# Queries and keys of a hybrid attention block projected with features on partitions, the scale of a query taken into the exponential

## The chip, the cores and the metric

The kernel runs as one program on one core of a Trainium2 chip. A core has five engines that work side by side, each through its own instructions in order: TensorE (PE in the profile; PEld is its weight load), VectorE (DVE), ScalarE (ACT), GpSimd (POOL) and SyncE (SP, which here issues transfers). They meet in the on-chip memories SBUF (128 partitions) and PSUM (128 partitions, banks of 512 float32) and wait for each other by semaphores. The metric is the device time of one execution in microseconds (us), as the median of several runs.

## The reference

A decoder block for 512 tokens of width 1024, in float32. What matters here is the sparse attention branch, one of two that run on the same normalised input:

```python
q = _rms_norm(q.reshape(B, S, ATTN_HEADS, ATTN_HEAD_DIM), attn_q_norm[l])
k = _rms_norm(k.reshape(B, S, ATTN_HEADS, ATTN_HEAD_DIM), attn_k_norm[l])
...
scores = jnp.einsum('bqhs,bqh->bqs', head_scores, wib) * IDX_HEADS ** -0.5
_, sel = lax.top_k(scores, topk)
...
logits = jnp.einsum('bqhd,bqkhd->bhqk', qb, k_sel).astype(f32) * scale
logits = logits + jnp.transpose(bias, (0, 3, 1, 2))
probs = jax.nn.softmax(logits, axis=-1).astype(v.dtype)
```

There are 8 heads of 64 features. Each head's query and key of a token is divided by the root mean square of its 64 features and multiplied by a gain per feature. An indexer scores the keys of each query, and each query attends to its 128 best keys.

## The kernel before

Every matrix product is made from three float32r products: activations and weights are split into a rounded part (`_hi`, `xnh`) and a remainder (`_lo`, `xnl`). The normalised input stands in SBUF with features on partitions. Weights stream in as chunks of 128x1024: SP issues the transfer into `w_raw`, ACT writes the rounded part `w_hi` (L241), and POOL (from the 18th chunk on every third one DVE) subtracts to get `w_lo` (L245). `w_hi` and `w_lo` have three buffers each.

Two helpers make products. `dense_t` keeps weights as the stationary operand, streams 512 tokens in one instruction and leaves features by tokens. `dense_k` keeps 128 tokens as the stationary operand, streams 256 columns of weights and leaves tokens by features. Queries, keys and values go through `dense_k` in that order, two calls of 256 columns each, from four chunks each.

For queries and keys each 128x256 piece of a result goes through `head_rms`. ACT copies it out of PSUM into `qraw` and squares it, DVE sums each head's 64 squares (L449), adds epsilon (L450), POOL raises to the power -0.5 (L452), and DVE multiplies the piece by that scale, one for each token and head (L453). Later, in `rest`, PE turns the piece over (`flip`, a transpose through the identity, L169), ACT writes the rounded part with the gain, and DVE the remainder (L465); keys get two more ACT copies (L467, L468). So the two flips of a piece wait for the chain ACT, DVE, POOL, DVE.

On the same DVE, at the same time, the indexer's choice runs. `scores` adds eight heads for each of three blocks of queries (256, 384 and 512 keys; L416 and L420, from `relu` tiles of ACT). `select` then makes 16 rounds for each block, each a search for the eight largest (L432) and their replacement (L433), and ends with a mask (L435). A block of `attention` needs its mask (`keep`); the first block needs none. Attention takes 32 units (four blocks by eight heads): PE makes logits, DVE adds a bias table `toep` and takes the maximum (L523 in the first block, L526 and L527 after it, L533 the sign), ACT takes the exponential (L534), PE flips it, and PE multiplies by values.

PE's order is written by hand: `Streams.run` hands PE to the part with the lowest rank that is due, by a clock of estimated PE times and by named signals; the delay `rms` in `L` says how long after its piece a `rest` may come. The order on the other engines is made by a scheduler with a timeline of its own. Each engine then executes strictly in that order.

## Time and profile before

| What | Value |
| --- | --- |
| Median of 3 runs | 963.98 us (963.55 to 964.72) |
| Profiled execution | 964.03 us, span of its trace 962.2 us |
| PE busy in the span | 915.0 us (95%) |
| DVE busy in the span | 435.9 us (45%) |
| ACT, POOL busy in the span | 350.6 us (36%), 372.3 us (39%) |

Shares over the whole span hide the stages: an engine that is busy for 45% of all can be the one that everything waits for during a tenth of it. The 40 slices of the page and busy times by window show this. "Idle before" is what an engine waited for just before an instruction. A waiting instruction holds up all behind it on its engine. A duration in the trace can hold a wait for a port that no semaphore shows, so durations of one kind are compared with each other.

### The profile page before, as it was taken

How to read it: one execution, taken by the hardware profiler on the slowest of the kernel's cores; microseconds unless marked ns; L12 is line 12 of the kernel's file. 1: busy time of each engine (PE TensorE's matmuls, PEld its weight loads, DVE VectorE, ACT ScalarE, POOL GpSimd, SP SyncE). 2: the span in 40 equal slices, each digit the busy share in tenths (PEclk: the TensorE clock that was granted, in tenths of full speed). 3: DMA queues.
4: the chain of work that ended last, by engine and by line, in shares of the span. 5: the costliest groups of instructions: out<-in, count | busy, mean ns of one | idle time of the engine just before them, and what ended most of it. 6: DMA issues, size and time to landing. Idle time of an engine off the chain costs nothing.

```text
span 962.2 us, 13991 instructions
## 1 busy us (share of the span) xinstructions
PE 915.0 (95%) x5670; PEld 779.0 (81%) x5670; DVE 435.9 (45%) x847; ACT 350.6 (36%) x596; POOL 372.3 (39%) x253
## 2 busy tenths in 40 slices
PE   6998777999999999999997999999999999999998
PEld 4997776888777778787886899888888888888886
DVE  5289999677466635765533715211111111101111
ACT  5454466544453433333323424332232323212120
POOL 6445441101357334444413733344444444432321
PEclk9998888999998999999998999999999999999999
DMA  6321232211212121011042222332223323223331
GB/s 230 80 89 44 67 88 66 66 45 44 77 45 66 44 81 53 24 45 44 23 143 77 88 88 69 95 100 88 99 98 92 106 88 110 88 95 102 132 110 44
DMA packets 24033, 77.80 MB, mean 81 GB/s; under 512 B 2726, under 2 KB 4223, under 8 KB 23969
## 3 DMA queue, kind: packets, MB, share of 16 engines
q1 hardware_dynamic: 20832, 72.56, 23.4%
q10 hardware_dynamic: 3136, 4.36, 1.6%
q8 instruction: 44, 0.72, 0.3%
q14 instruction: 21, 0.16, 0.1%
HBM read 74.53 MB, written 2.38 MB: 80 GB/s over the span
## 4 chain that ended last, share of the span: by engine, by line
PE 84%; DVE 11%; issue 2%; ACT 1%; POOL 1%; DMA 0%; ACTq 0%; DVEq 0%; POOLq 0%
PE ps_d L162 60%; PE ps_c L162 11%; PE ps_i L162 10%; DVE score L433 2%; PE ps_c L169 2%; DVE max L432 2%; DVE qraw L453 1%; DVE score L420 1%; DVE qs L465 1%; PE ps_i L169 1%; DVE qss L449 1%; DVE lg L527 1%; POOL w_lo L245 0%; DVE kl L465 0%; DVE xs L330 0%
## 5 line engine op out<-in xcount | busy, mean ns | idle before, releaser
L245 POOL TENSOR_TENSOR w_lo<-w_raw,w_hi 128x1024 fp32r<-128x1024 f32 (+1 forms) x94 | 222.0, 2364 | 387.5 <-ACT w_hi L241 383.9
L241 ACT ACTIVATE w_hi<-w_raw 128x1024 fp32r<-128x1024 f32 x129 | 136.6, 1059 | 346.5 <-PE ps_d L162 219.4
L162 PE MATMUL ps_d<-hnl,w_hi 128*128 128x512 f32 (+1 forms) x368 | 139.9, 380 | 0.4 <-DVE hnl L338 0.4
L162 PE MATMUL ps_d<-hnh,w_hi 128*128 128x512 f32 (+1 forms) x368 | 139.9, 380 | 0.0
L162 PE MATMUL ps_d<-hnh,w_lo 128*128 128x512 f32 (+1 forms) x368 | 139.8, 380 | 0.0
L162 PE MATMUL ps_d<-xnh,w_hi 128*128 128x512 f32 (+2 forms) x296 | 124.5, 420 | 0.0
L162 PE MATMUL ps_d<-xnh,w_lo 128*128 128x512 f32 (+2 forms) x296 | 112.8, 381 | 0.0
L162 PE MATMUL ps_d<-xnl,w_hi 128*128 128x512 f32 (+2 forms) x296 | 112.4, 380 | 0.0
L245 DVE TENSOR_TENSOR w_lo<-w_raw,w_hi 128x1024 fp32r<-128x1024 f32 x37 | 47.6, 1286 | 126.8 <-ACT w_hi L241 126.2
L1045 DVE TENSOR_TENSOR gsig<-ps_d,gsig 128x512 f32<-128x512 f32 x22 | 15.2, 692 | 157.6 <-PE ps_d L162 156.9
L162 PEld LDWEIGHTS ps_d<-hnl,w_hi 128*128 128x128 f32 x368 | 69.2, 188 | 13.4 <-DVE hnl L338 0.6
L162 PEld LDWEIGHTS ps_d<-hnh,w_lo 128*128 128x128 f32 x368 | 69.2, 188 | 13.2
L162 PEld LDWEIGHTS ps_d<-hnh,w_hi 128*128 128x128 f32 x368 | 69.2, 188 | 13.2
L162 PEld LDWEIGHTS ps_d<-xnh,w_hi 128*128 128x128 f32 x296 | 57.2, 193 | 10.0 <-issue 2.6
L162 PEld LDWEIGHTS ps_d<-xnh,w_lo 128*128 128x128 f32 x296 | 56.8, 192 | 10.5
L162 PEld LDWEIGHTS ps_d<-xnl,w_hi 128*128 128x128 f32 x296 | 57.2, 193 | 8.1 <-issue 1.9
L162 PE MATMUL ps_d<-w_hi,xnh 128*128 128x256 f32 x192 | 58.9, 307 | 0.0
L162 PE MATMUL ps_d<-w_lo,xnh 128*128 128x256 f32 x192 | 57.7, 301 | 0.0
L162 PE MATMUL ps_d<-w_hi,xnl 128*128 128x256 f32 x192 | 57.6, 300 | 0.0
L1049 POOL TENSOR_TENSOR ul<-gsig,uh 128x512 fp32r<-128x512 f32 x22 | 31.6, 1434 | 25.3 <-ACT uh L1048 25.3
L162 PEld LDWEIGHTS ps_d<-w_hi,xnh 128*128 128x128 f32 x192 | 40.8, 212 | 0.4
L162 PEld LDWEIGHTS ps_d<-w_lo,xnh 128*128 128x128 f32 x192 | 40.5, 211 | 0.4
(283 smaller groups left out, 1814.9 us busy)
## 6 DMA issues: line engine op xcount, KB each, us to landing
w_raw<-in_stream_dram SPq DMA_DIRECT2D x129, 512.0 KB, 3.5
xa<-in_x_dram SPq DMA_DIRECT2D x4, 512.0 KB, 6.5
ht<-in_x_dram ACTq DMA_DIRECT2D x8, 256.0 KB, 3.2
out_dram<-ht SPq DMA_DIRECT2D x8, 256.0 KB, 2.0
toep<-bias_table ACTq DMA_DIRECT2D x8, 128.0 KB, 2.6
gain<-in_rows_dram ACTq DMA_DIRECT2D x2, 256.0 KB, 4.2
con<-in_consts_dram SPq DMA_DIRECT2D x1, 321.0 KB
bias_table<-tab ACTq DMA_DIRECT2D x1, 276.0 KB
```

The lines of the kernel that those rows point to most:

```text
L162: nc.tensor.matmul(o, w, r, **kw)
L169: nc.tensor.transpose(o, src, idn)
L241: nc.scalar.activation(hi, raw, AF.Copy)
L245: eng.tensor_sub(lo[:, o:o + n_], raw[:, o:o + n_], hi[:, o:o + n_])
L420: nc.vector.scalar_tensor_tensor(sc, r, w, sc, op0=OP.mult, op1=OP.add)
L432: nc.vector.max(m8, sc)
L433: nc.vector.match_replace(sc, m8, sc, TAKEN)
L449: nc.vector.tensor_reduce(ss, hv(sq), axis=AX.X, op=OP.add)
L453: nc.vector.tensor_mul(hv(raw), hv(raw), rs[:, :, None].to_broadcast([128, 4, 64]))
L465: nc.vector.scalar_tensor_tensor(at_(lo, b), p2[a], gain[a], at_(hi, a), op0=OP.mult, op1=OP.subtract)
L1045: nc.vector.tensor_mul(g, pu, g)
L1049: nc.gpsimd.tensor_sub(ul, g, uh)
```

## The change

Queries and keys go through `dense_t`, a pair of chunks at a time, so that they come out of PE as features by tokens. Nothing of a query is flipped. A query isn't scaled: PE sums the squares of each head by a product with a 128x2 matrix of ones (`head_sums`, four instructions), DVE adds epsilon, and after the fourth piece POOL makes two 128x32 tables, the power -0.5 (the scale) and 0.5 (its inverse). The scale goes into the exponential as its `scale` operand and into the negated maximum, and the bias table is multiplied by the inverse before it is added. The first block's fused add and maximum becomes two instructions. A key's sums go through POOL as 128x8, ACT spreads them over 512 columns, PE flips that tile (four flips), and DVE multiplies the raw key by it, straight from PSUM. The remainder of a key is then the difference of two SBUF tiles. Attention waits for all queries and keys at once, where it waited block by block.

```diff
@@ -86,7 +86,7 @@
-L = dict(norm=3.0, normed=1.3, score=0.4, pick=0.15, rms=14.5, attn=0.6, attn_n=0.15, attn_out=2.0, sig=0.3,
+L = dict(norm=3.0, normed=1.3, score=0.4, pick=0.15, rms=6.5, sums=2.5, attn=0.6, attn_n=0.15, attn_out=2.0, sig=0.3,
          prep=5.0, knorm=6.5, bonus=6.0, mat=0.5, mats=2.8, inv_u=3.25, inv_t=1.4, inv_r=1.4, inv_n=0.9, inv_e=1.8,
...
@@ -225,8 +225,10 @@
...
-    mhalf = cp.tile([128, 8], F32, name="mhalf")
-    nc.gpsimd.memset(mhalf, -0.5)
+    half = cp.tile([128, 64], F32, name="half")
+    mhalf = half[:, 0:8]
+    nc.gpsimd.memset(half[:, 0:32], -0.5)
+    nc.gpsimd.memset(half[:, 32:64], 0.5)
@@ -438,39 +440,74 @@
     qs_, kh_, kl_ = big("qs", F32R), big("kh", F32R), big("kl", F32R)
-    pairs = lambda a: a.rearrange("q (p e) t -> q p e t", e=2)
     vt = [bp.tile([128, S], F32, name="vt", tag=tag, bufs=n) for tag, n in (("uu", 1), ("tt", 1), ("rr", 2), ("rr", 2))]
-    def head_rms(g, gain, name, t, ps):
-        raw, sq = [q for q in unit("qraw").rearrange("q (a b) -> a q b", a=2)]
-        nc.scalar.activation(raw, ps, AF.Copy)
-        nc.scalar.activation(sq, raw, AF.Square, scale=N ** -0.5)
-        ss = small("qss", 4)
-        nc.vector.tensor_reduce(ss, hv(sq), axis=AX.X, op=OP.add)
-        nc.vector.tensor_scalar(ss, ss, RMS_EPS, None, op0=OP.add)
-        rs = small("qrs", 4)
-        nc.gpsimd.tensor_tensor(rs, ss, mhalf[:, 0:4], op=OP.pow)
-        nc.vector.tensor_mul(hv(raw), hv(raw), rs[:, :, None].to_broadcast([128, 4, 64]))
+    qss = cp.tile([128, NT, H], F32, name="qss")
+    qrs = cp.tile([128, 2, NT, H], F32, name="qrs")
+    def split_heads(j, src, gain, hi, lo, twice):
+        for e in range(2):
+            a, b, h = slice(64 * e, 64 * e + 64), slice(64 - 64 * e, 128 - 64 * e), 2 * j + e
+            if gain is None:
+                nc.scalar.activation(hi[a, h], src[a], AF.Copy)
+                nc.vector.tensor_sub(lo[b, h], src[a], hi[a, h])
+            else:
+                nc.scalar.activation(hi[a, h], src[a], AF.Copy, scale=gain[a])
+                nc.vector.scalar_tensor_tensor(lo[b, h], src[a], gain[a], hi[a, h], op0=OP.mult, op1=OP.subtract)
+            if twice:
+                nc.scalar.activation(hi[b, h], src[a], AF.Copy)
+                nc.scalar.activation(lo[a, h], lo[b, h], AF.Copy)
+    def head_sums(sq):
+        ps = bank("i")
+        for t in range(NT):
+            mm(ps[:, 2 * t:2 * t + 2], sq[:, t * 128:t * 128 + 128], cst("blk"), start=True, stop=True)
+        return ps[:, 0:8]
+    def queries(j, ps):
+        sq = unit("qsq")
+        nc.scalar.activation(sq, ps, AF.Square, scale=N ** -0.5)
+        split_heads(j, ps, qg, qs_, qs_, False)
         def rest():
+            s = head_sums(sq)
+            nc.vector.tensor_scalar(qss[:, :, 2 * j:2 * j + 2], s.rearrange("q (t h) -> q t h", h=2), RMS_EPS, None,
+                                    op0=OP.add)
+            if j == 3:
+                flat = lambda q: q.rearrange("q t h -> q (t h)")
+                for i in range(2):
+                    nc.gpsimd.tensor_tensor(flat(qrs[:, i]), flat(qss), half[:, i * 32:i * 32 + 32], op=OP.pow)
+                st.signal("q", 5.0)
+            yield 0.0
+        st.add(3, rest(), L["sums"])
+    def keys(j, ps):
+        raw, sq = unit("kraw"), unit("ksq")
+        nc.scalar.activation(sq, ps, AF.Square, scale=N ** -0.5)
+        nc.scalar.activation(raw, ps, AF.Copy, scale=pc("kn"))
+        def rest():
+            s = head_sums(sq)
+            ss, rs = small("qss", 8), small("qrs", 8)
+            nc.vector.tensor_scalar(ss, s, RMS_EPS, None, op0=OP.add)
+            nc.gpsimd.tensor_tensor(rs, ss, mhalf, op=OP.pow)
+            nc.scalar.activation(hv(sq), rs[:, :, None].to_broadcast([128, 8, 64]), AF.Copy)
+            yield L["rms"]
             ps = bank("i")
-            for j in range(2):
-                flip(ps[:, j * 128:j * 128 + 128], raw[:, j * 128:j * 128 + 128], ident)
-            p2 = ps[:, 0:256].rearrange("q (j t) -> q j t", j=2)
-            for e in range(2):
-                a, b = slice(64 * e, 64 * e + 64), slice(64 - 64 * e, 128 - 64 * e)
-                at_ = lambda z, q: pairs(z)[q, 2 * g:2 * g + 2, e, t * 128:t * 128 + 128]
-                hi, lo = (qs_, qs_) if name == "q" else (kh_, kl_)
-                nc.scalar.activation(at_(hi, a), p2[a], AF.Copy, scale=gain[a])
-                nc.vector.scalar_tensor_tensor(at_(lo, b), p2[a], gain[a], at_(hi, a), op0=OP.mult, op1=OP.subtract)
-                if name == "k":
-                    nc.scalar.activation(at_(hi, b), p2[a], AF.Copy, scale=gain[a])
-                    nc.scalar.activation(at_(lo, a), at_(lo, b), AF.Copy)
-            if g == 1:
-                st.signal(f"{name}{t}", 1.0)
+            for t in range(NT):
+                flip(ps[:, t * 128:t * 128 + 128], sq[:, t * 128:t * 128 + 128], ident)
+            nc.vector.tensor_mul(raw, raw, ps)
+            split_heads(j, raw, None, kh_, kl_, True)
+            if j == 3:
+                st.signal("k", 4.0)
             yield 0.0
-        st.add(3, rest(), L["rms"])
+        st.add(3, rest(), L["sums"])
@@ -479,6 +516,8 @@
...
         yield "v"
+        yield "q"
+        yield "k"
         for g in range(4):
...
@@ -495,8 +534,6 @@
...
                 if h == 0:
-                    yield f"q{i}"
-                    yield f"k{i}"
                     if i:
...
@@ -519,19 +556,20 @@
...
         mx = small("mx", 4)
+        scale, root = [qrs[:, j, i, h:h + 1] for j in range(2)]
         if i == 0:
-            nc.vector.tensor_tensor_reduce(lg, ps, toep[h][:, 128:256], 1.0, NEG, op0=OP.add, op1=OP.max,
-                                           accum_out=mx[:, 0:1])
+            nc.vector.scalar_tensor_tensor(lg, toep[h][:, 128:256], root, ps, op0=OP.mult, op1=OP.add)
+            nc.vector.tensor_reduce(mx[:, 0:1], lg, axis=AX.X, op=OP.max)
         else:
-            nc.vector.tensor_add(lg[:, n - 256:], ps[:, n - 256:], toep[h])
+            nc.vector.scalar_tensor_tensor(lg[:, n - 256:], toep[h], root, ps[:, n - 256:], op0=OP.mult, op1=OP.add)
             nc.vector.tensor_tensor_reduce(lg[:, n - 256:], lg[:, n - 256:], keep[i][:, n - 256:], 1.0, 2 * NEG,
...
         m = mx[:, 1:2] if i > 1 else mx[:, 0:1]
-        nc.vector.tensor_scalar(mx[:, 2:3], m, -1.0, None, op0=OP.mult)
-        nc.scalar.activation(lg, lg, AF.Exp, bias=mx[:, 2:3], accum_out=den[:, h:h + 1])
+        nc.vector.tensor_scalar(mx[:, 2:3], m, scale, -1.0, op0=OP.mult, op1=OP.mult)
+        nc.scalar.activation(lg, lg, AF.Exp, scale=scale, bias=mx[:, 2:3], accum_out=den[:, h:h + 1])
         return lg
@@ -959,9 +997,13 @@
...
         st.add(1, select())
-        for gain, name in ((qg, "q"), (pc("kn"), "k")):
-            for g in range(2):
-                yield from dense_k(xn, lambda t, ps: head_rms(g, gain, name, t, ps))
+        for part in (queries, keys):
+            for j in range(4):
+                if j % 2 == 0:
+                    wt = chunk(4, 256) + chunk(4, 256)
+                ps = bank("d")
+                yield from dense_t(ps, wt, slice((j % 2) * 128, (j % 2) * 128 + 128), xn)
+                part(j, ps)
         for g in range(2):
...```

On DVE, where a key's piece is finished among the rounds of the choice: before, each piece of 256 columns brings a scaling from SBUF (L453) and four remainders from PSUM (L465). `qraw` is a piece, `score_614` the scores of the second block of queries.

```order
L465 SCALAR_TENSOR_TENSOR kl_135<-ps_i_1418,fst_72,kh_134 64x2x128
L433 MATCH_REPLACE score_614<-max8_1100,score_614 128x384
L465 SCALAR_TENSOR_TENSOR kl_135<-ps_i_1429,fst_72,kh_134 64x2x128
L450 TENSOR_SCALAR qss_1392<-qss_1392 128x4
L432 MAX max8_1112<-score_614 128x8
L465 SCALAR_TENSOR_TENSOR kl_135<-ps_i_1418,fst_72,kh_134 64x2x128
L453 TENSOR_TENSOR qraw_1380<-qraw_1380,qrs_1386 128x256
L433 MATCH_REPLACE score_614<-max8_1112,score_614 128x384
L453 TENSOR_TENSOR qraw_1389<-qraw_1389,qrs_1395 128x256
L465 SCALAR_TENSOR_TENSOR kl_135<-ps_i_1429,fst_72,kh_134 64x2x128
```

The same place after: `kraw` is a raw key of 128 features by 512 tokens, `ps_i` the flipped scale, `kh` the rounded part.

```order
L504 TENSOR_TENSOR kraw_926<-kraw_926,ps_i_1035 128x512
L434 MAX max8_968<-score_593 128x8
L435 MATCH_REPLACE score_593<-max8_968,score_593 128x384
L455 TENSOR_TENSOR kl_136<-kraw_926,kh_135 64x512
L434 MAX max8_977<-score_593 128x8
L455 TENSOR_TENSOR kl_136<-kraw_926,kh_135 64x512
L435 MATCH_REPLACE score_593<-max8_977,score_593 128x384
L434 MAX max8_1003<-score_593 128x8
L435 MATCH_REPLACE score_593<-max8_1003,score_593 128x384
L497 TENSOR_SCALAR qss_1086<-ps_i_1081 128x8
```

The scaling moved from SBUF alone to a PSUM operand, the remainder from a PSUM operand to SBUF alone, and there are fewer of both between the rounds.

On POOL, at the keys before, two small powers stand between the weight remainders:

```order
L452 TENSOR_TENSOR qrs_1136<-qss_1133,mhalf_94 128x4
L452 TENSOR_TENSOR qrs_1145<-qss_1142,mhalf_94 128x4
L245 TENSOR_TENSOR w_lo_1403<-w_raw_1400,w_hi_1402 128x1024
L452 TENSOR_TENSOR qrs_1187<-qss_1184,mhalf_94 128x4
L452 TENSOR_TENSOR qrs_1196<-qss_1193,mhalf_94 128x4
L245 TENSOR_TENSOR w_lo_1516<-w_raw_1513,w_hi_1515 128x1024
```

After, the two tables of the queries (L483) come in one place, ahead of a weight remainder and of the first key's power (L498):

```order
L247 TENSOR_TENSOR w_lo_987<-w_raw_984,w_hi_986 128x1024
L483 TENSOR_TENSOR qrs_142<-qss_141,half_94 128x32 x2
L247 TENSOR_TENSOR w_lo_993<-w_raw_990,w_hi_992 128x1024
L498 TENSOR_TENSOR qrs_955<-qss_954,half_94 128x8
L247 TENSOR_TENSOR w_lo_1132<-w_raw_1129,w_hi_1131 128x1024
```

The weight remainder that the second half of the third key's product needs (`w_lo_993`) and the first key's scale now stand behind both tables.

On PE, inside the fourth key's product (`ps_d_1062`), the third key's sums and the second key's flips stand after the change, four instructions each for a whole piece of 512 tokens:

```order
L162 MATMUL ps_d_1062<-xnh_118,w_lo_987 128x512
L162 MATMUL ps_i_1081<-con_87,ksq_1059 128x2 x4
L162 MATMUL ps_d_1062<-xnh_119,w_hi_992 128x512
L162 MATMUL ps_d_1062<-xnl_121,w_hi_992 128x512
L162 MATMUL ps_d_1062<-xnh_119,w_lo_993 128x512
L169 MATMUL ps_i_1097<-fst_72,ksq_981 128x128 x4
```

Before, two flips for each of 16 pieces stood there, between products of 256 columns:

```order
L162 MATMUL ps_d_1399<-w_lo_1403,xnh_117 128x256
L162 MATMUL ps_d_1399<-w_hi_1402,xnl_119 128x256
L169 MATMUL ps_i_1467<-fst_72,qraw_1181 128x128 x2
L169 MATMUL ps_i_1478<-fst_72,qraw_1190 128x128 x2
L162 MATMUL ps_d_1399<-w_hi_1402,xnh_117 128x256
```

What PE stops for is a flip of the piece itself before, and of a tile of scales after.

## Rows read from the trace of the kernel before

**Rows 1.** The page: PE's busy tenths in 40 slices of 24 us, and the engines of the chain of work that ended last.

```profile
PE   6998777999999999999997999999999999999998
PE 84%; DVE 11%; issue 2%; ACT 1%; POOL 1%; DMA 0%; ACTq 0%; DVEq 0%; POOLq 0%
```

**Rows 2.** Busy time of each engine by window: the stage from the first score to the end of the choice, its middle, and the stretch after it. Columns: window, length, busy us of each engine with its instructions in brackets, then the granted clock of TensorE as a share of full speed, the share of the DMA engines and GB/s.

```profile
48.77:168.48 119.71, 97.48 (x678) 93.10 (x677) 113.10 (x269) 66.12 (x147) 44.58 (x28) 0.89 0.23 70
75.00:150.00 75.00, 54.26 (x383) 52.22 (x382) 72.53 (x173) 38.17 (x86) 30.25 (x20) 0.85 0.24 71
168.48:400.00 231.52, 227.60 (x1527) 186.00 (x1526) 145.91 (x322) 98.64 (x188) 85.18 (x67) 0.99 0.17 54
```

**Rows 3.** Who waited for whom, 50 to 165 us (total us, times, longest), and one of these waits in PE's timeline (start, duration, what; in brackets the idle time before it and its releaser).

```profile
PE ps_i L169 <- ACT kh L467: 11.6, 4, 4.9
PE ps_i L169 <- DVE qs L465: 10.0, 3, 5.4
...
108.84 1.08 PE L169 MATMUL ps_i<-fst,qraw 128*128 128x128 f32 x4 [5.45 <-DVE qs L465]
```

**Rows 4.** Groups by line and shape, 50 to 165 us: all DVE work of `head_rms`. Columns: count, busy us and mean ns of one, idle time before.

```profile
L453 DVE TENSOR_TENSOR qraw<-qraw,qrs 128x256 f32<-128x256 f32 x16 | 17.4, 1090 | 0.1
L465 DVE SCALAR_TENSOR_TENSOR kl<-ps_i,fst,kh 64x256 fp32r<-64x256 f32 x16 | 7.6, 483 | 0.9 <-ACT kh L464 0.3
L465 DVE SCALAR_TENSOR_TENSOR qs<-ps_i,der,qs 64x256 fp32r<-64x256 f32 x16 | 7.6, 483 | 0.5
L449 DVE TENSOR_REDUCE qss<-qraw 128x4 f32<-128x256 f32 x16 | 6.3, 410 | 0.0
L450 DVE TENSOR_SCALAR qss<-qss 128x4 f32<-128x4 f32 x16 | 2.2, 162 | 0.1
```

**Rows 5.** DVE's timeline (start, duration): two instructions of one kind, one short and one long, the instruction after the short one, two other long ones, and a search; then POOL's timeline at the long ones and at the search, and the last weight remainder of the stage.

```profile
109.61 0.41 DVE L453 TENSOR_TENSOR qraw<-qraw,qrs 128x256 f32<-128x256 f32 x1
109.93 0.08 DVE L433 MATCH_VALUE_LOAD score<-max,score 128x8 f32 x1
65.63 2.29 DVE L453 TENSOR_TENSOR qraw<-qraw,qrs 128x256 f32<-128x256 f32 x1
55.31 3.04 DVE L420 SCALAR_TENSOR_TENSOR score<-relu,widx,score 128x256 f32<-128x256 f32 x2 [1.23 <-ACT relu L419]
137.22 2.08 DVE L435 TENSOR_SCALAR score<-score 128x384 f32<-128x384 f32 x1
114.34 0.56 DVE L432 MAX8 max<-score 128x8 f32<-128x384 f32 x1
...
55.08 2.39 POOL L245 TENSOR_TENSOR w_lo<-w_raw,w_hi 128x1024 fp32r<-128x1024 f32 x1 [4.95 <-ACT w_hi L241]
65.25 2.40 POOL L245 TENSOR_TENSOR w_lo<-w_raw,w_hi 128x1024 fp32r<-128x1024 f32 x1
114.34 2.40 POOL L245 TENSOR_TENSOR w_lo<-w_raw,w_hi 128x1024 fp32r<-128x1024 f32 x1 [4.64 <-ACT w_hi L241]
136.69 2.40 POOL L245 TENSOR_TENSOR w_lo<-w_raw,w_hi 128x1024 fp32r<-128x1024 f32 x1 [9.29 <-ACT w_hi L241]
142.22 2.40 POOL L245 TENSOR_TENSOR w_lo<-w_raw,w_hi 128x1024 fp32r<-128x1024 f32 x1 [3.13 <-ACT w_hi L241]
```

**Rows 6.** Groups by line and shape, whole span, DVE: the operations nearest to the added ones (a multiply and add from PSUM, a small addition from PSUM, a product with a PSUM operand, a difference of SBUF tiles).

```profile
L389 DVE SCALAR_TENSOR_TENSOR zk<-ps_d,der,zk 128x511 f32<-128x511 f32 x4 | 3.0, 744 | 0.0
L645 DVE TENSOR_SCALAR kss<-ps_i 128x8 f32<-128x8 f32 x4 | 0.7, 167 | 0.9 <-PE ps_i L162 0.8
L558 DVE TENSOR_TENSOR ytile<-ps_i,den 128x512 f32<-128x512 f32 x4 | 2.7, 684 | 2.4 <-PE ps_i L162 2.4
L999 DVE TENSOR_TENSOR yr<-zv,yr 128x512 fp32r<-128x512 f32 x4 | 2.5, 687 | 0.7 <-ACT yr L998 0.7
```

**Rows 7.** PE's timeline (start, duration): two neighbours with 256 columns, two with 512, and seven sums of squares by a 128x2 matrix.

```profile
47.10 0.28 PE L162 MATMUL ps_d<-w_hi,xnl 128*128 128x256 f32 x1
47.22 0.28 PE L162 MATMUL ps_d<-w_hi,xnh 128*128 128x256 f32 x1
...
271.19 0.40 PE L162 MATMUL ps_d<-xnh,w_lo 128*128 128x512 f32 x1
271.43 0.40 PE L162 MATMUL ps_d<-xnh,w_hi 128*128 128x512 f32 x1
...
269.85 0.92 PE L162 MATMUL ps_i<-con,sq 128*128 128x2 f32 x7
```

**Rows 8.** Groups by line and shape, POOL: powers of 4 and of 8 columns.

```profile
L452 POOL TENSOR_TENSOR qrs<-qss,mhalf 128x4 f32<-128x4 f32 x16 | 17.1, 1083 | 30.7 <-DVE qss L450 30.7
L647 POOL TENSOR_TENSOR krs<-kss,mhalf 128x8 f32<-128x8 f32 x4 | 8.9, 2225 | 4.4 <-DVE kss L645 4.4
L884 POOL TENSOR_TENSOR yrs<-yst,mhalf 128x8 f32<-128x8 f32 x4 | 6.6, 1641 | 5.2 <-DVE yst L882 5.2
```

**Rows 9.** DVE's timeline: the first score, and the last instruction of the choice.

```profile
48.77 0.48 DVE L416 TENSOR_SCALAR score<-ps_c,widx 128x256 f32<-128x256 f32 x1
168.06 0.42 DVE L435 TENSOR_SCALAR score<-score 128x512 f32<-128x512 f32 x1
```

**Rows 10.** Groups by line and shape, 165 to 250 us, DVE: the bias in the first block (fused with the maximum) and in the later ones.

```profile
L523 DVE CUSTOM_DVE_ANT_0 lg<-ps_c,toep 128x128 f32<-128x128 f32 x6 | 1.7, 290 | 1.5 <-ACT pt L546 1.5
L526 DVE TENSOR_TENSOR lg<-ps_c,toep 128x256 f32<-128x256 f32 x24 | 10.0, 417 | 8.2 <-PE ps_c L162 7.3 <-ACT lg L534 0.9
```

2 lines of the change are left out of this document (1 added, 1 removed).

## The prediction

> **What bounds the kernel now.** I read the 40 slices first. PE is busy nearly throughout, except for a dip from the fourth to the seventh slice, and the chain that ended last is PE for 84% and DVE for 11% [rows 1]. So most of the span is PE's own pace, and DVE owns a share that must lie in one place. The windows find it [rows 2]: from the first score to the end of the choice, 48.8 to 168.5 us [rows 9], DVE is busy for 113.1 of 119.7 us. In the 75 us in the middle it is busy for 72.5, while PE is busy for 54.3 at a granted clock of 0.85, a mean of the levels 1.2 and 2.4 GHz. After 168.5 us PE is busy for 227.6 of 231.5 us at a clock of 0.99. PE's own waits name the link [rows 3]: 21.6 us, nearly all before flips, released by DVE's remainder or an ACT copy that stands behind one. Flips wait because DVE, executing in order, reaches sums, scalings and remainders only among the rounds of the choice. I conclude that this stage ends when DVE has done its list, and that what is taken from that list, up to PE's own limit, comes off the end of the program, since PE sets the pace behind it.
>
> **What leaves DVE.** All its work in `head_rms` is 17.4 + 7.6 + 7.6 + 6.3 + 2.2 = 41.1 us [rows 4]. Not all is computing. One scaling took 0.41 us and another 2.29 us [rows 5]. The long one began 0.4 us into a weight remainder on POOL and ended just after it. A score and a mask did the same (55.3 and 137.2 us), while a search that began together with a remainder took 0.56 us. So 16 bare scalings are 16 x 0.41 = 6.6 us, and 10.8 us of the 17.4 is waiting for POOL. The bare work that leaves is 41.1 - 10.8 = 30.3 us. Neighbours overlap: the instruction behind a 0.41 us scaling starts 0.32 us after it [rows 5], and 48 of the 80 that leave are of that short kind, so I take off 48 x 0.09 = 4 us: 26 us.
>
> **What comes to DVE.** Eight remainders of a query, 64x512 from PSUM, at 0.744: 6.0 us. Eight small additions from PSUM at 0.167: 1.3 us. Four scalings of a key with a PSUM operand at 0.684: 2.7 us. Eight remainders of a key from two SBUF tiles at 0.687: 5.5 us [rows 6]. The sum is 15.5 us, less about 1 us of the same overlap, 14.5 us. In the stage's last few attention units the fused add and maximum (0.29 us [rows 10]) becomes two instructions; no row has a maximum of 128 columns, so I bound the extra one by nothing and by the 0.41 us of a sum over 256 [rows 4], take 0.25 for its length, and count 0.5 us for two or three units. Bare saving: 26 - 14.5 - 0.5 = 11 us.
>
> **What becomes of the waits for POOL.** Ten weight remainders run on POOL from 55.1 to 142.2 us [rows 5]. Eight of them held DVE up: 10.8 us at scalings, 3.04 - 2 x 0.48 = 2.1 us at the score, and about 1.7 us at the mask, 14.6 us in all. An instruction with two SBUF tiles as inputs is held, and one mask of a single tile; a search is not, and one with a PSUM operand shows no long case (the means of L465, L389 and L558 lie at their bare times [rows 4, 6]). After the change the scalings read PSUM and can't be held, but the scores still can, and eight key remainders now can, which could not before. By the new order about three weight remainders fall among the scores, which come about one a microsecond, so I count three holds of 2 us. Three or four find nothing but searches and PSUM readers. Four fall among the keys' remainders, of which one or two a hold apart: I count 2 us. That is 8 us instead of 14.6, a gain of 6.6 us. Ends: one hold of 2 us (gain 12.6) and as much as now (gain 0).
>
> The Trainium skill (SBUF — State Buffer, Who interferes with whom) says that a DVE instruction with two SBUF inputs contends with a GpSimd instruction that reads SBUF, and that whichever starts first has the shared port for its whole length. The trace agrees: 2.29 us instead of 0.41. Read as a rule against this change, it opens the keys' remainders to all four late windows; if each held one for 2 us, the sum would be 6 us smaller than mine.
>
> **New waits.** A key's scale takes a longer road: PE sums, DVE addition, POOL power, ACT spread, PE flip, DVE scaling. In DVE's order some nine rounds of the choice stand between a key's addition and its scaling, and PE's next stop waits on the same road, so DVE should rarely run dry. The unknown is the queries' two 128x32 powers: from 1.08 us for 4 columns and 1.64 to 2.23 us for 8 [rows 8], a straight line gives 5 to 9 us each. They hold a weight remainder and the first key's power for 10 to 18 us. With 10 to 12 us the first key's flip still comes before DVE asks for it; with 18 us DVE waits about 4 us. I count 1 us, ends 0 and 4.
>
> **What PE gains by itself.** Starts of 256-column products lie 0.12 us apart and those of 512 columns 0.24 us [rows 7]. So 384 x 0.12 = 46.1 us become 192 x 0.24 = 46.1 us: half the instructions, the same time. Added are 32 sums at 0.92 / 7 = 0.13 us, 4.2 us, and 16 flips of 32 leave, 2 to 3 us at 0.13 to 0.17 us each. PE's own total hardly changes. It was busy for 97.5 us in the stage at a mean clock of 0.89 [rows 2], which I estimate at some 87 us at full clock. DVE's list is 113.1 - 41.1 - 2.1 - 1.7 + 14.5 + 0.5 + 8 = 91 us, still the longer one. All the gain is DVE's. ACT has 66 us of work in 120 us [rows 2] and loses some; no transfer is added, removed or moved past another except the loads of `toep`, which wait for buffers of the first two keys and should land before the first unit.
>
> **The sum.** 11 + 6.6 - 1 = 16.6, some 17 us, against the profiled 964.0 us (span 962.2 us), which is the median within 0.1 us: 947 us. Ends: 11 + 12.6 = 23.6 us less gives 940; 11 + 0 - 4 = 7 us less gives 957.
>
> **The rivals.** First, DVE's list shrinks so far, because almost no remainder meets POOL, that PE at a full clock becomes the pace of the stage: 20 to 27 us less, 937 to 944. For it: PE idles less, and the clock was 0.85 where it idled. Against it: without any hold DVE's list is still 83 us, and with the 6.6 us that it sat idle or between instructions in the stage (119.7 - 113.1) 90 us, no shorter than PE's.
> Second, the key road and POOL eat the gain: both powers at 9 us, each late window holding a remainder, so that PE again waits at flips: 4 to 10 us less, 954 to 960. For it: POOL's line grows from 8 to 32 columns without a row. Against it: only one of the four keys stands right behind them.
> Third, slower: the attention units. Each of the 32 gets a multiply and add (0.48 us for 256 columns by L465 [rows 4]) for a plain add (0.417 [rows 10]), and the first eight one instruction more. That is 24 x 0.06 + 8 x 0.25 = 3.5 us of DVE, in a stretch where DVE is busy for 146 of 231 us [rows 2], so it should hide. It decides if a unit's chain gets later than PE's next flip of it, two units on: at 0.66 us for each of 32 units it costs 21 us and gives 968. Nothing in the rows shows a lack of slack of that size.
> Fourth, nothing measurable: PE's pace was the limit of the stage all along and the waits only move; 963 to 965. The idle PE in rows 2 and 3 speaks against it.
>
> **How the numbers follow.** Forecast case (8 to 20 us less) 60%, first rival 17%, second 16%, no change 3%, slower 4%. About 0.2% (2 us) is what a measurement of this kernel can tell from no change. Faster 0.93, same 0.03, slower 0.04. The range 939 to 957 holds the forecast case with the near parts of its two neighbours.
>
> **What would show it.** Right: between the first score and the end of the choice the profile after shows about 103 us instead of 119.7, DVE still over 90% busy there, PE idle before flips of `ksq` rather than of `qraw`, long DVE instructions only where POOL subtracts, key scalings at 0.7 us. After the choice, the same length of stage as before. Wrong: DVE idle by more than 5 us in the stage (the key road), PE idle in the attention units (third rival), or a stage shorter by far more than DVE's list.

## The result, and the profile after

The changed kernel takes 947.38 us (median of 4 runs, 945.72 to 948.14), the kernel before on the same chip 963.76 us (962.37 to 964.72): a ratio of 0.9829 with a 95% interval of 0.981 to 0.9848, or 16.4 us less. The profiled execution is the fastest of the four, 945.72 us with a span of 943.6 us. In the experiments some executions of a kernel, of the one before too, take about 10 us longer (the three profiles of such an execution, of *more sums*, *queries alone* and *both*, have a granted clock of 0.93 to 0.95 between 180 and 400 us, the others 0.98 to 1.00); the times called undisturbed leave them out, the ratios beside them do not.

The page of the changed kernel, the lines of [rows 1]:

```profile
PE   6999799999999999999998999999999999999998
PE 82%; DVE 13%; issue 2%; ACT 1%; POOL 1%; DMA 0%; ACTq 0%; POOLq 0%; DVEq 0%
```

The dip that PE had in the fourth to seventh slice is down to one digit, the fifth. The share of DVE in the chain rose from 11% to 13% though, so the chain alone would not tell that DVE was relieved. Windows of the same kernel: the stage from the first score (47.50 us) to the end of the choice, what lies behind it up to 380 us, and 45 to 180 us, which holds the stage in every kernel of this study (columns as in [rows 2]):

```profile
47.50:146.20 98.70, 92.32 (x529) 80.77 (x529) 93.35 (x210) 55.28 (x93) 45.38 (x18) 0.95 0.27 82
146.20:380.00 233.80, 226.71 (x1522) 184.47 (x1521) 148.74 (x328) 103.14 (x192) 84.08 (x67) 1.00 0.18 55
...
45.00:180.00 135.00, 127.64 (x732) 110.19 (x731) 119.20 (x289) 75.54 (x143) 53.98 (x22) 0.96 0.26 76
```

The stage took 119.71 us and takes 98.70. DVE is still busy for 95% of it. PE, which worked for 81% of the stage before, now works for 94%, at a granted clock of 0.95 instead of 0.89. PE's waits between 45 and 180 us in the changed kernel, to be held against [rows 3]:

```profile
PE ps_d L162 <- POOL w_lo L247: 3.4, 1, 3.4
PE ps_c L169 <- ACT lg L572: 1.3, 3, 0.7
PE ps_i L162 <- ACT ksq L491: 1.3, 1, 1.3
PE ps_c L162 <- DVE score L418: 1.1, 1, 1.1
PE ps_i L169 <- ACT ksq L499: 0.2, 1, 0.2
```

This is the view to remember. The 21.6 us at flips are gone but for 0.2; what is left is 7.3 us, against 22.1 in the same window of the kernel before (the two rows of [rows 3] and 0.5 at a score). The largest single stop is new. POOL's timeline of the changed kernel shows where it is from:

```profile
87.08 10.84 POOL L483 TENSOR_TENSOR qrs<-qss,half 128x32 f32<-128x32 f32 x2 [3.69 <-DVE qss L478]
97.88 2.35 POOL L247 TENSOR_TENSOR w_lo<-w_raw,w_hi 128x1024 fp32r<-128x1024 f32 x1
```

Both powers of the queries stand ahead of a weight remainder, which ends at 100.23 us, and PE's next product starts at 100.28.

Groups by line and shape, 45 to 165 us, DVE: a group of scores, then what came, for [rows 4 and 6], with the two instructions of the first attention block (L561, L562):

```profile
L422 DVE SCALAR_TENSOR_TENSOR score<-relu,widx,score 128x384 f32<-128x384 f32 x7 | 7.6, 1081 | 0.0
L455 DVE TENSOR_TENSOR kl<-kraw,kh 64x512 fp32r<-64x512 f32 x8 | 7.3, 916 | 0.3
L458 DVE SCALAR_TENSOR_TENSOR qs<-ps_d,der,qs 64x512 fp32r<-64x512 f32 x8 | 6.0, 750 | 1.2 <-ACT qs L457 1.0
...
L561 DVE SCALAR_TENSOR_TENSOR lg<-toep,qrs,ps_c 128x128 f32<-128x128 f32 x8 | 2.7, 342 | 1.0 <-PE ps_c L162 1.0
L504 DVE TENSOR_TENSOR kraw<-kraw,ps_i 128x512 f32<-128x512 f32 x4 | 2.7, 676 | 0.0
...
L562 DVE TENSOR_REDUCE mx<-lg 128x1 f32<-128x128 f32 x8 | 2.3, 283 | 0.2
...
L478 DVE TENSOR_SCALAR qss<-ps_i 128x8 f32<-128x8 f32 x4 | 0.6, 160 | 0.1
```

DVE's timeline, the instructions that a weight remainder on POOL held up (for [rows 5]), and the last one of the choice (for [rows 9]):

```profile
59.23 2.18 DVE L422 SCALAR_TENSOR_TENSOR score<-relu,widx,score 128x384 f32<-128x384 f32 x1
63.51 2.36 DVE L422 SCALAR_TENSOR_TENSOR score<-relu,widx,score 128x384 f32<-128x384 f32 x1
78.80 1.25 DVE L424 TENSOR_TENSOR score<-score,con 128x128 f32<-128x128 f32 x1
113.03 1.57 DVE L437 TENSOR_SCALAR score<-score 128x384 f32<-128x384 f32 x1
116.68 2.53 DVE L455 TENSOR_TENSOR kl<-kraw,kh 64x512 fp32r<-64x512 f32 x1
145.78 0.42 DVE L437 TENSOR_SCALAR score<-score 128x512 f32<-128x512 f32 x1
```

Where the gain lies is read from a landmark behind the stage, the last of `zk`'s four mixings, in DVE's timeline of the kernel before (first fence) and of the changed one (second):

```profile
207.65 0.75 DVE L389 SCALAR_TENSOR_TENSOR zk<-ps_d,der,zk 128x511 f32<-128x511 f32 x1
```

```profile
188.56 0.74 DVE L391 SCALAR_TENSOR_TENSOR zk<-ps_d,der,zk 128x511 f32<-128x511 f32 x1
```

The landmark comes 19.1 us earlier, the end of the span 18.6 us. The first score already came 1.3 us earlier [rows 9], in a stretch that the change does not touch. So some 17.8 us were won between the first score and the landmark, and 0.5 us was given back behind it.

### The profile page after: what moved, and what is told of

Same layout as the page of the kernel before. It is cut to its first block, busy times and chain, and to the rows that moved or that the text cites. A ratio compares the mean times of both kernels' runs of the same rounds, so it can differ in the third digit from the quotient of the medians.

```text
span 943.6 us, 13578 instructions
## 1 busy us (share of the span) xinstructions
PE 909.3 (96%) x5526; PEld 764.5 (81%) x5526; DVE 418.0 (44%) x795; ACT 344.2 (36%) x548; POOL 373.1 (40%) x244
## 2 busy tenths in 40 slices
PE   6999799999999999999998999999999999999998
## 4 chain that ended last, share of the span: by engine, by line
PE 82%; DVE 13%; issue 2%; ACT 1%; POOL 1%; DMA 0%; ACTq 0%; POOLq 0%; DVEq 0%
PE ps_d L162 59%; PE ps_c L162 11%; PE ps_i L162 9%; DVE score L435 3%; DVE max L434 2%; PE ps_c L169 2%; DVE score L422 1%; DVE lg L565 1%; DVE kl L455 1%; DVE qs L458 1%; POOL w_lo L247 1%; PE ps_i L169 0%; PE ps_d L169 0%; DVE xs L332 0%; DMA grow<-in_rows_dram 0%
## 5 line engine op out<-in xcount | busy, mean ns | idle before, releaser
L247 POOL TENSOR_TENSOR w_lo<-w_raw,w_hi 128x1024 fp32r<-128x1024 f32 (+1 forms) x94 | 222.0, 2363 | 386.0 <-ACT w_hi L243 382.6
L162 PE MATMUL ps_d<-xnh,w_hi 128*128 128x512 f32 (+2 forms) x360 | 149.5, 415 | 0.0
L162 PE MATMUL ps_d<-xnh,w_lo 128*128 128x512 f32 (+2 forms) x360 | 137.6, 382 | 3.4 <-POOL w_lo L247 3.4
L162 PE MATMUL ps_d<-hnl,w_hi 128*128 128x512 f32 (+1 forms) x368 | 139.9, 380 | 0.4 <-DVE hnl L340 0.4
L162 PE MATMUL ps_d<-hnh,w_hi 128*128 128x512 f32 (+1 forms) x368 | 140.0, 380 | 0.0
L162 PE MATMUL ps_d<-hnh,w_lo 128*128 128x512 f32 (+1 forms) x368 | 139.8, 380 | 0.0
L162 PE MATMUL ps_d<-xnl,w_hi 128*128 128x512 f32 (+2 forms) x360 | 136.8, 380 | 0.0
L247 DVE TENSOR_TENSOR w_lo<-w_raw,w_hi 128x1024 fp32r<-128x1024 f32 x37 | 46.0, 1244 | 127.1 <-ACT w_hi L243 126.5
L162 PEld LDWEIGHTS ps_d<-xnh,w_lo 128*128 128x128 f32 x360 | 68.3, 190 | 16.9 <-POOL w_lo L247 3.9
L162 PEld LDWEIGHTS ps_d<-hnl,w_hi 128*128 128x128 f32 x368 | 69.2, 188 | 13.5 <-DVE hnl L340 0.6
L162 PEld LDWEIGHTS ps_d<-hnh,w_lo 128*128 128x128 f32 x368 | 69.2, 188 | 13.2
L162 PEld LDWEIGHTS ps_d<-hnh,w_hi 128*128 128x128 f32 x368 | 69.2, 188 | 13.1
L162 PEld LDWEIGHTS ps_d<-xnh,w_hi 128*128 128x128 f32 x360 | 68.8, 191 | 11.4 <-issue 2.6
L162 PEld LDWEIGHTS ps_d<-xnl,w_hi 128*128 128x128 f32 x360 | 68.8, 191 | 9.8 <-issue 1.9
L797 POOL COPY rr<-eye 128x512 f16<-128x512 f16 x20 | 15.5, 780 | 47.8 <-PE ps_i L162 47.8
L162 PE MATMUL ps_d<-w_hi,mh 128*128 128x256 f32 x120 | 34.1, 284 | 0.0
L162 PE MATMUL ps_d<-w_hi,ml 128*128 128x256 f32 x120 | 34.0, 283 | 0.0
L162 PE MATMUL ps_d<-w_lo,mh 128*128 128x256 f32 x120 | 34.0, 283 | 0.0
L572 ACT ACTIVATE lg<-lg,mx,qrs 128x128 f32<-128x128 f32 (+3 forms) x32 | 20.9, 652 | 32.2 <-DVE mx L571 31.4
```

What stands on the lines that cost most here:

```text
L162: nc.tensor.matmul(o, w, r, **kw)
L247: eng.tensor_sub(lo[:, o:o + n_], raw[:, o:o + n_], hi[:, o:o + n_])
L572: nc.scalar.activation(lg, lg, AF.Exp, scale=scale, bias=mx[:, 2:3], accum_out=den[:, h:h + 1])
L797: nc.gpsimd.tensor_copy(two(R, 1), eye16.rearrange("q (g w s) -> q g w s", w=2, s=s)[:, None, :, 1] .to_broadcast([128, H, 64 // s, s]))
```

## The experiments

**The prediction's test comes out right in the main, so a harder one is needed.** DVE's share in the stage and the time came out as forecast, and the length of its list nearly (93.35 us, 91 forecast). Three signs did not. The stage got 21.0 us shorter, to 98.7 and not to about 103 us. What follows it, where the same length was forecast, grew from 793.7 to 797.4 us, so not all that left the list came off the end. And PE's stops before flips of `ksq` are 0.2 us. The prediction's theory is that the stage ends when DVE's list is done. The rival, close to its first rival, is that PE sets the pace throughout, and that the time before went into PE's stops at places in its fixed order. Two doses on DVE's list tell them apart.

*More sums.* Two sums per projected piece, behind its square, into a tile that nobody reads (shown for queries; the same lines stand in `keys`):

```diff
+        for _ in range(2):
+            nc.vector.tensor_reduce(small("extra", 8), hv(sq), axis=AX.X, op=OP.add)
```

> The changed kernel with 16 more sums on DVE in the stage, two of 0.69 us behind each of the eight projected pieces (their result is used by nobody, and they read one SBUF tile, so POOL can't hold them). DVE-list theory: the stage is as long as DVE's list, so the time grows by nearly all of it, 16 x 0.69 = 11.0 us less 1.4 us of overlap, 9.6 us: 957 us. Rival (the gain came from PE's fewer instructions and flips, DVE has room now): 0 to 3 us more, 947 to 950 us.

*Twelve rounds.* Each block chooses 96 of its keys and not 128:

```diff
-            for _ in range(TOPK // 8):
+            for _ in range(TOPK // 8 - 4):
```

> The changed kernel with 12 rounds of the choice instead of 16 in each block (96 of the 128 keys are chosen, so the output differs). That takes 4 x (0.99 + 1.25 + 1.51) = 15 us off DVE's list in the stage. DVE-list theory: the stage shrinks from 98.7 us until PE's own pace, some 88 us, stops it: 9 to 11 us less, 936 to 938 us; a full 15 us less (932 us) would mean that PE's limit lies lower than I think. Rival (PE sets the stage already): within 2 us of 947 us.

More sums: 947.8 us (946.1 to 949.5 undisturbed). Twelve rounds: 947.8 us (946.9 to 948.5; ratio to the kernel before 0.9793, 0.9736 to 0.9851). The mask of the last block, which ends the choice, in DVE's timeline of the first kernel, and of the second:

```profile
157.36 0.42 DVE L437 TENSOR_SCALAR score<-score 128x512 f32<-128x512 f32 x1
```

```profile
128.44 2.60 DVE L437 TENSOR_SCALAR score<-score 128x512 f32<-128x512 f32 x1
```

The doses reached the list. With first scores at 48.50 and 48.66 us, the stage took 109.3 and 82.4 us instead of 98.7: 10.6 more and 16.3 less. The time moved by less than 1 us in both. In the changed kernel the end of DVE's list binds nobody. The stage is bounded by two instructions of DVE itself, so its length follows DVE's list whatever paces the program. The first reader of that last mask shows why nothing waits: it is the first unit of the last attention block, in DVE's timeline of the kernel before at

```profile
217.56 2.30 DVE L527 CUSTOM_DVE_ANT_0 lg<-lg,score 128x256 f32<-128x256 f32 x1
```

which is 49 us behind the end of the choice at 168.48 [rows 9]. The kernel before had shown it all along; a run on that kernel follows (*flips later*).

*More products*, the mirror on PE: five more issues of each piece's first product.

```diff
+                for _ in range(5):
+                    mm(ps, wt[0][0][:, 0:128], xn[0][0], start=True, stop=False, skip_group_check=True)
+                    yield 0.0
                 yield from dense_t(ps, wt, slice((j % 2) * 128, (j % 2) * 128 + 128), xn)
```

> The kernel after, with 40 more products on PE in the projections of queries and keys: the first 128x512 product of each of the eight pieces is issued five more times, with start, so each rewrites the same bank. 40 x 0.24 us = 9.6 us of PE at full clock, the mirror of the 16 sums that were added to DVE. Theory that PE sets the pace of the stage (what the change removed were PE's stops): the kernel after gets 8 to 10 us longer, 955 to 958 us. Theory of the prediction that DVE's list sets the end of the stage: PE's estimate rises from 87 to 97 us, against DVE's 91 us forecast and the 98.7 us that the stage took, so at most 0 to 2 us, 947 to 950 us.

951.8 us (949.6 to 954.0), 4.5 us more than the changed kernel, between the two forecasts. PE's stops fell from 7.3 to 4.4 us, and the one before `w_lo` is gone, which leaves 9.6 - 2.9 = 6.7 us. The clock between 45 and 180 us rose from 0.96 to 0.99; that this gave back the other 2 us is likely, not shown. So a dose on PE costs where the same dose on DVE doesn't, but not in full: the added work fills stops first.

**Is it the stops?** Two kernels change DVE's list or PE's order in the kernel before, and two take half of the change.

*Scaling on ACT*: the kernel before, its DVE scalings moved to ACT.

```diff
-        nc.vector.tensor_mul(hv(raw), hv(raw), rs[:, :, None].to_broadcast([128, 4, 64]))
+        for h in range(4):
+            cs = slice(h * 64, h * 64 + 64)
+            nc.scalar.activation(raw[:, cs], raw[:, cs], AF.Copy, scale=rs[:, h:h + 1])
```

> The kernel before with the scaling of a raw piece moved from DVE to ACT (four instructions of 64 columns for each piece, 64 in all, some 18 us of ACT work); products, flips and all else as before. It takes the 17.4 us of scalings and their holds off DVE. DVE-list theory: 6.6 us of bare work less overlap and most of 10.8 us of holds go, of which a part comes back at scores and masks: 9 to 15 us less than before, 949 to 955 us. Rival (PE's products and flips made the gain): within 3 us of 964 us, or slower since flips now wait for four ACT instructions.

959.1 us undisturbed (957.1 to 959.4; ratio 0.9905, 0.9869 to 0.9942), 5.4 us less than the kernel before on that chip: between the two forecasts, 9 to 15 us less (DVE theory) and within 3 us (rival). The stage took 107.8 instead of 119.7 us, 11.9 us less, of which the time shows less than half. PE's waits between 45 and 180 us:

```profile
PE ps_i L169 <- ACT kh L469: 10.8, 4, 6.8
PE ps_i L169 <- DVE qs L467: 7.1, 4, 3.7
PE ps_c L162 <- DVE score L416: 1.3, 1, 1.3
```

Its stops at flips shrank only from 21.6 to 17.9 us. All stops together fell by 2.9 us in the window. In the profile the last mixing of `zk` comes 4.1 us earlier (203.57 us) and the end of the span 6.2 us, so a part of the gain lies behind the stage and is not explained.

*Flips later*: the kernel before with one of the planner's due times changed, no instruction added or removed.

```diff
-L = dict(norm=3.0, normed=1.3, score=0.4, pick=0.15, rms=14.5, attn=0.6,
+L = dict(norm=3.0, normed=1.3, score=0.4, pick=0.15, rms=21.0, attn=0.6,
```

> The kernel before, with one number of the planner changed: the flips of a scaled query or key are put 21.0 instead of 14.5 planner units behind its projection. No instruction is added or removed on any engine, only PE's, ACT's and DVE's order moves. Theory that PE's stops at flips are the cost: the scaled rows are there earlier before their flips, the 21.6 us of stops before flips shrink by a third to two thirds, 7 to 14 us less, 950 to 957 us. Theory that DVE's list sets the end: the list is the same 113 us, so no change within 1 us, 963 to 965 us.

957.8 us undisturbed, against 963.6 for the kernel before on that chip (ratio 0.9931, 0.9887 to 0.9976), at DVE's same work (121.9 us busy between 45 and 180 us, 120.6 before). PE's waits in that window:

```profile
PE ps_i L169 <- DVE qs L465: 9.6, 4, 4.1
PE ps_i L169 <- ACT kh L467: 5.9, 4, 2.3
PE ps_c L169 <- ACT lg L534: 1.7, 1, 1.7
PE ps_c L162 <- DVE score L416: 0.6, 1, 0.6
```

Stops at flips fell from 21.6 to 15.5 us, all stops by 4.3 us and the time by 5.8: short of the expected 7 to 14, but far from the nothing that the DVE theory asked for. The choice meanwhile ended later, with this mask in DVE's timeline:

```profile
174.77 0.42 DVE L435 TENSOR_SCALAR score<-score 128x512 f32<-128x512 f32 x1
```

The first score comes at 48.76 us as before, so DVE's stage is 6.7 us longer (126.4 us) and the program 5.8 us shorter. That settles it for the kernel before too: the end of DVE's list did not set the end of the program. A third of the change's gain is to be had by moving PE's flips alone.

*Queries alone* and *keys alone*: each half of the change, the other half's code as before (shown: where the queries alone call it).

```diff
-        for part in (queries, keys):
+        for part in (queries,):
...
+        for g in range(2):
+            yield from dense_k(xn, lambda t, ps: head_rms(g, pc("kn"), "k", t, ps))
```

> Half of the change: the queries are projected as features by tokens, with their scale in the exponential; the keys stay as before (projected as tokens by features, scaled in place, flipped, eight flip places). Theory that PE's stops at flips are what the time went into: the stops released by a query's remainder, 10.0 us in the kernel before, go, those released by a key's copy, 11.6 us, stay or shrink a little: 8 to 12 us less than before, 952 to 956 us. Theory that DVE's list sets the end: the queries' half of the bare work that leaves (13 us) less what comes (8 x 0.744 + 4 x 0.167 = 6.6 us) and half of the holds gone: 8 to 11 us less, 953 to 956 us. The two agree on the time; they differ on where: the first expects PE's stops in this stage to fall by about as much as the time, whatever length DVE's list has.

> The other half: the keys are projected as features by tokens with a flipped tile of scales; queries and the attention units stay as before, with the maximum fused into the addition. Theory that PE's stops are the cost: the stops at key copies (11.6 us) go and 1 to 2 us of stops before flips of ksq come; the queries' 10.0 us stay: 8 to 11 us less than before, 953 to 956 us. Theory that DVE's list sets the end: 13 us of bare work leaves and 2.7 + 5.5 + 0.7 - 0.5 = 8.4 us comes, and holds fall by some 2 us: 5 to 7 us less, 957 to 959 us.

Queries alone: ten runs, median 957.7 us, of which the five undisturbed lie at 949.5 to 951.8, their median 12.6 us below the kernel before on that chip (963.6 undisturbed); the last mixing of `zk` comes at 194.78 us, 12.9 us earlier. Keys alone: 949.4 to 952.0 undisturbed, about 14 us less, where 5 to 7 (DVE's list) or 8 to 11 (stops) were expected. Both forecasts were too small. PE's waits between 45 and 180 us with the queries alone, and with the keys alone:

```profile
PE ps_i L169 <- ACT kh L514: 7.9, 4, 4.4
PE ps_d L162 <- POOL w_lo L247: 1.8, 1, 1.8
PE ps_c L162 <- DVE score L418: 1.1, 1, 1.1
PE ps_c L169 <- ACT lg L582: 0.9, 2, 0.7
```

```profile
PE ps_i L169 <- DVE qs L493: 5.5, 3, 3.5
PE ps_i L162 <- DVE qs L493: 2.8, 1, 2.8
PE ps_i L162 <- ACT ksq L507: 1.2, 1, 1.2
PE ps_c L162 <- DVE score L418: 0.5, 1, 0.5
PE ps_c L169 <- ACT lg L587: 0.5, 1, 0.5
PE ps_i L169 <- DVE qss L513: 0.3, 1, 0.3
```

Either half took away more than its own stops: those at key copies shrank from 11.6 to 7.9 us though the keys were as before, and those at query remainders from 10.0 to 8.3. The halves add up to 27 us and together give 16.4. The reading that fits, not tested apart, is that whichever comes second finds part of its stops gone, and that the whole has the new one behind the powers.

**What is left to gain.**

*Tables late*: the changed kernel, the two powers of 128x32 moved behind the last key's power.

```diff
-            if j == 3:
-                flat = lambda q: q.rearrange("q t h -> q (t h)")
...
             nc.gpsimd.tensor_tensor(rs, ss, mhalf, op=OP.pow)
+            if j == 3:
+                flat = lambda q: q.rearrange("q t h -> q (t h)")
...
```

> The changed kernel with the two 128x32 powers of the queries moved on POOL from behind the last query to behind the last key's power. PE's stop of 3.4 us for the weight remainder that stands behind them should go. DVE-list theory: PE's stop is hidden by DVE's list, so the time stays within 1.5 us of 947 us (the attention units may start a few us later for their scales, which would cost the same in another place). Rival (PE's stops set the stage): 3 to 4 us less, 943 to 944 us.

947.7 us undisturbed (945.9 to 948.6), and nothing follows: although written later, the powers stand at the same place in POOL's order (they start at 87.26 us, 87.08 before the edit), and the trace has the same 3.4 us stop.

*Powers spread*: eight small powers instead of two long ones.

```diff
-                    nc.gpsimd.tensor_tensor(flat(qrs[:, i]), flat(qss), half[:, i * 32:i * 32 + 32], op=OP.pow)
+            for i in range(2):
+                nc.gpsimd.tensor_tensor(qrs[:, i, :, 2 * j:2 * j + 2], qss[:, :, 2 * j:2 * j + 2],
+                                        half[:, i * 32:i * 32 + 8].rearrange("q (t h) -> q t h", h=2), op=OP.pow)
```

> The kernel after, with the queries' powers in eight pieces: two of 128x4x2 on POOL behind each pair of heads (about 1.64 us each by the 128x8 row) instead of two of 128x32 (5.44 us each) behind the last pair. Theory that PE sets the pace: the 3.4 us that PE waits for the weight remainder behind the two long powers goes, 2 to 3.5 us less than the kernel after, 944 to 945.5 us. Theory that DVE's list sets the end: that list is not touched, so no change, 947 to 948 us; a third possibility is that the same POOL work spread out holds other remainders up and the stop only moves, also 947 to 948 us, with a PE wait for a remainder in another place.

944.1 us undisturbed (943.97 to 944.47), 3 us less, as the stops theory forecast, though not quite by its road. The 3.4 us stop went, but a stop of 1.3 us before a key's square grew to 4.5. PE's largest wait, and ACT's timeline:

```profile
PE ps_i L162 <- ACT ksq L491: 4.5, 1, 4.5
```

```profile
103.64 0.63 ACT L499 ACTIVATE ksq<-qrs 128x512 f32<-128x512 f32 x1 [5.57 <-POOL qrs L498]
```

ACT stood 5.6 us at another key's spread, waiting for POOL's power, ahead of that square. The sum of stops fell only from 7.3 to 5.6 us; the clock rose from 0.96 to 0.99.

*PSUM operands*: two tiles less as second SBUF inputs.

```diff
-                    r = unit("relu")[:, :n]
-                    nc.scalar.activation(r, ps, AF.Relu)
-                    nc.vector.scalar_tensor_tensor(sc, r, w, sc, op0=OP.mult, op1=OP.add)
+                    nc.scalar.activation(ps, ps, AF.Relu)
+                    nc.vector.scalar_tensor_tensor(sc, ps, w, sc, op0=OP.mult, op1=OP.add)
...
-            nc.vector.tensor_mul(raw, raw, ps)
-            split_heads(j, raw, None, kh_, kl_, True)
+            nc.vector.tensor_mul(ps, raw, ps)
+            split_heads(j, ps, None, kh_, kl_, True)
```

> The kernel after, with two tiles kept in PSUM: the rectified products of a score are written back to their bank, and a scaled key goes to its bank, so that the fused score and the key's remainder have one SBUF operand and POOL can't hold them. Of the 7.3 us in which weight remainders held DVE in the stage, the two at scores of 2.18 and 2.36 us and the one at a key's remainder of 2.53 us go, some 5.5 us of holds beyond the bare times. Theory that DVE's list sets the end: 4 to 5.5 us less than the kernel after, 942 to 943.5 us. Theory that PE sets the pace: 0 to 1 us less, 946.5 to 948 us, and PE's stops as they were.

941.3 us (940.3 to 941.5 undisturbed), 6 us less. Here the stops theory's expectation failed, and the other's (942 to 943.5) was nearly met. The groups of DVE show that the holds went (45 to 165 us):

```profile
L454 DVE TENSOR_TENSOR kl<-ps_i,kh 64x512 fp32r<-64x512 f32 x8 | 5.5, 689 | 0.4 <-ACT kh L453 0.2
...
L421 DVE SCALAR_TENSOR_TENSOR score<-ps_c,widx,score 128x384 f32<-128x384 f32 x7 | 4.3, 609 | 0.1
```

against means of 916 and 1081 ns. But DVE's list was shown above not to matter by its length, and PE's stops fell with the holds, from 7.3 to 3.8 us: without them the queries' powers, which wait for DVE's additions, start at 85.0 instead of 87.1 us, although the first score comes 1.8 us later (49.30), and the 3.4 us stop behind them shrinks to 0.3. POOL's timeline:

```profile
85.01 10.84 POOL L482 TENSOR_TENSOR qrs<-qss,half 128x32 f32<-128x32 f32 x2 [0.50 <-DVE qss L477]
```

I had expected the stops to stay. Counted from the first score the powers start 3.9 us earlier. The holds ahead of them in the changed kernel, two at scores more than 20 us earlier and a smaller one at 78.80, come to 4.3 us beyond their bare times, so the holds at scores were part of that stop. The keys' half of the edit acts behind the powers and can't have moved them; the two halves were not run apart.

*Both*, the two edits together:

> The kernel after with both edits that took time off it: rectified scores and scaled keys kept in PSUM, and the queries' powers in eight pieces of 128x4x2. Theory that PE's stops are what is left to gain: of the 7.3 us of stops between 45 and 180 us in the kernel after some 2 to 4 us stay, so 939 to 942 us, no more than 2 us less than with the PSUM tiles alone (941.4 us), since the 3.4 us stop was already gone there. If the two gains added up (4 to 6 and 3 us), 938 us.

938.0 us (936.1 to 939.1 undisturbed; ratio 0.9709, 0.9665 to 0.9753), the best version of the study, 9 us below the changed kernel: the two gains added up, where the stops theory had expected 939 to 942. PE's waits between 45 and 180 us:

```profile
PE ps_c L169 <- ACT lg L571: 1.1, 3, 0.7
PE ps_c L162 <- DVE score L421: 0.5, 1, 0.5
PE ps_i L169 <- DVE qss L496: 0.4, 1, 0.4
```

**All kernels side by side**, from 45 to 180 us: the sum of PE's waits in that window, the mean clock and DVE's busy time from the windows; then DVE's stage, from the first score to the end of the choice, and the median of the undisturbed runs.

| kernel | PE's stops, us | clock | DVE busy, us | DVE's stage, us | time, us |
|---|---|---|---|---|---|
| before | 22.1 | 0.90 | 120.6 | 119.7 | 964 |
| scaling on ACT | 19.2 | 0.91 | 113.8 | 107.8 | 959.1 |
| flips later | 17.8 | 0.92 | 121.9 | 126.4 | 957.8 |
| queries alone | 11.7 | 0.94 | 119.9 | 105.6 | 951.0 |
| keys alone | 10.8 | 0.94 | 118.2 | 110.4 | 949.5 |
| more sums | 8.4 | 0.96 | 120.8 | 109.3 | 947.8 |
| changed | 7.3 | 0.96 | 119.2 | 98.7 | 947.4 |
| twelve rounds | 6.9 | 0.96 | 106.9 | 82.4 | 947.8 |
| powers spread | 5.6 | 0.99 | 117.8 | 99.4 | 944.1 |
| PSUM operands | 3.8 | 0.99 | 116.7 | 94.8 | 941.3 |
| both | 2.0 | 1.00 | 118.7 | 94.6 | 938.0 |

The time falls with PE's stops line by line, but for one step of 0.4 us, and neither DVE column orders it. (The kernel with more products, whose PE has 9.6 us more to do, isn't in it.) From the first row to the last, 20.1 us fewer stops go with 26 us less: the stops, and about a quarter more, in step with the clock, which is lower where PE stops. What the clock adds can be read behind one stop of the kernel before, the one of 5.45 us that ends at 108.84 us [rows 3], in windows ahead of it, just behind it and after that (columns as in [rows 2]):

```profile
100.00:103.10 3.10, 3.10 (x28) 3.10 (x28) 3.10 (x14) 1.97 (x5) 1.91 (x2) 1.00 0.02 5
108.90:114.20 5.30, 5.30 (x25) 5.18 (x26) 5.05 (x13) 2.83 (x5) 0.81 (x1) 0.50 0.02 3
114.40:120.00 5.60, 5.60 (x49) 5.60 (x49) 5.39 (x17) 1.81 (x7) 2.95 (x2) 1.00 0.29 94
```

PE is busy in all of each, and in the second its clock is granted at half, 1.2 GHz: products of 256 columns start 0.21 us apart there and 0.12 us apart in the other two. The four flips and 22 products from 108.84 us take 5.5 us and would take some 3.1 at the pace of the first window, so by this estimate the stop of 5.45 us cost about 2.4 us more than its length. Behind the changed kernel's stop of 3.4 us the clock reads 0.51 from 100.3 to 104.9 us. This was not summed over all stops, so that the whole quarter is the clock's is not shown.

## Why the prediction was right, and where not

The number was right: 947 us forecast, 947.38 measured. So were most terms of the sum, but the step that joins them to the end of the program was not, and so the number was luck.

- **What bounds the stage.** That "this stage ends when DVE has done its list, and that what is taken from that list, up to PE's own limit, comes off the end of the program" is the step that failed. More sums and twelve rounds moved the end of that list by +10.6 and -16.3 us against the first score and the time by less than 1; with the flips later the list ended 6.7 us later than before and the program 5.8 us earlier. PE paced the kernel before and after, and what cost was that its flips stood in its order ahead of inputs that DVE and ACT delivered late. DVE's length mattered only through how late those inputs came.
- **Why the number came out all the same.** The list lost 113.1 - 93.35 = 19.8 us. The forecast had two figures for that: 11 + 6.6 = 17.6 by the sum, and 22 by the list of 91 us, which leaves out the 4 us taken off for overlap. The terms came out as forecast or near it: remainders of a query 0.750 us (0.744 taken), a key's scaling 0.676 (0.684), small additions 0.16 (0.167), the extra maximum 0.283 (0.25). PE's stops lost 14.8 us, and 3 us more of the 17.8 up to the landmark fit the clock. That the two amounts are alike is a coincidence: with the scaling on ACT the stage got 11.9 us shorter, and the program 5.4.
- **The holds.** Beyond their bare times (0.61, 0.61, 0.29, 0.35 and 0.69 us in the groups where nothing holds them, the mask between those of 256 and 512 columns) the five held instructions lost 7.3 us; 8 were counted. Of the eight key remainders one was held, as counted, and not four, as the rule's reading had it. That holds can be taken away is worth 6 us, as the PSUM operands show, though by way of PE's stops. The Trainium skill (SBUF — State Buffer, Who interferes with whom) also says that a DVE `tensor_scalar`, with one input, can enter a mode that contends with GpSimd. The masks agree: 0.42 us for 512 columns at 145.78 us in the changed kernel, where no weight remainder runs on POOL, and 2.60 us in the kernel with twelve rounds, where the mask begins at 128.44, 0.09 us into a weight remainder on POOL.
- **New waits.** Counted at 1 us, with ends 0 and 4, and looked for at DVE. The powers took 5.44 us each, inside the 5 to 9, but the wait fell on PE: 3.4 us behind the weight remainder, and 1.5 us before `ksq`. The prediction saw the remainder queued behind the powers and did not ask who waits for it.
- **PE's own total.** That the products cost the same was right, and so was the note that PE's total hardly changes. The estimate of 87 us as PE's length of the stage was of work alone; with 6.4 us of stops and a clock of 0.95 PE fills the 98.7 us as DVE's list does, and so the two could not be told apart by the length of the stage.
- **The first rival** (PE becomes the pace, 937 to 944) had the right engine, and its 937 to 944 us are reached once most stops are gone, with two more edits (938.0). It was wrong that PE *becomes* the pace, and that the change removes nearly all stops.
- **The second rival** (the key road and POOL eat the gain, 954 to 960) asked for powers of 9 us and a held remainder in each late window; the powers took 5.44 us and one remainder was held. PE did wait behind the powers, but for weights and not at flips. DVE's idle time in the stage, 98.70 - 93.35 = 5.35 us, is just over the 5 us named as a sign of this road, but it was 6.6 before.
- **The third rival** is answered: units with one instruction more cost about 0.5 us behind the stage, not 21. **The fourth** was half right: PE was the pace all along, but its stops could be taken away.
